# A fused encoder layer: softmax division on rows by VectorE and GpSimd, residual stores from ScalarE, embedding loads from GpSimd, the embedding stage's sums spread otherwise

## The chip, the cores and the metric

The kernel runs on one core of a Trainium2 chip. The metric is device time in microseconds (us). Its engines work from queues of their own: TensorE (PE in the profile, its weight loads PEld), VectorE (DVE), ScalarE (ACT), GpSimd (POOL) and SyncE (SP, which here only issues transfers). An engine takes its instructions strictly in the order of its queue, and a wait on a semaphore holds up everything queued behind it.

## The reference, cut to what matters

One layer over x of 1024 tokens by 1024 features, all in float32:

```
u    = x @ W_in                                # projection
R    = bidirectional retention, 8 heads        # chunks of 128 tokens
A    = windowed attention, 8 query heads, 2 key/value heads, 128 tokens to each side
       e = exp(scores - m);  probs = e / (sum(e) + exp(sink - m));  out = probs @ v
h    = LN1(alpha * x + concat(R * silu(gate), A) @ W_out)
f    = (silu(h @ W_gate) * (h @ W_up)) @ W_down + sigmoid(h @ W_pg) * (p @ W_pe)
out  = LN2(alpha * h + f)
```

The division `e / (...)` and the gated embedding `sigmoid(h @ W_pg) * (p @ W_pe)` are the two places that most of the change is about.

## The kernel before, in words

Matrices are multiplied in tiles of 128 x 128 by 128 x 512. Each float32 operand is split into a high part and the remainder (`split`: ScalarE copies, L79, VectorE subtracts, L80), and three multiplications make one product (`mm3`, L83 to L85; `mm3c`, L288 to L290). Large products use a scheme with 7 products of sums of quarter matrices instead of 8 products of quarters. So there are always sums of operands to be made by VectorE and GpSimd ahead of a product, and sums of results behind it.

The stages, in time: the first projection (to about 49 us), the other projections (49 to 171), retention and attention together (171 to 420), the out projection with LN1 (420 to 515), the gated embedding (`ple`, 515 to 602), gate and up products of the feed-forward part (602 to about 1040) and the down product with LN2 (to the end).

**Order.** In the projections, in `ple` and in the feed-forward part all five queues follow the order of the program text (`manual_schedule`). In the attention stage only TensorE does so; the other four are ordered by a scheduler that estimates times. In the out projection a scheduler orders all five.

**Projections.** The 7 products of a pair of weight tiles run as 6, 5, 2, 7, 4, 3 (with 1 earlier). Products 4 to 7 use sums of x, kept split in the tiles `TX`: two of them in a pool of their own (`T`), two in slots that keys (`k`) and queries (`q`, `v`) need later. After products 5, 2, 7 and 4 of the last pair, `keys` (L330 to L341) and `queries` (L343) build the split keys and queries of the attention.

**Attention.** There are 4 pairs of heads, and for each pair 8 blocks of 128 queries. `scores(n)` multiplies queries and keys into a bank (L671, L672); VectorE adds the distance term and takes the maximum (L673); ScalarE takes exp with the row sum (L677); VectorE takes the reciprocal of the sum (L679); GpSimd multiplies the identity matrix by it, which gives two diagonal matrices `dg` (L681). `turn(n)` then multiplies each 128 x 128 block of e by its `dg` (L690): one matmul that transposes the block and divides it. ScalarE copies the result to `ptr` (L692), and `values(n)` multiplies it by v (L702). TensorE runs `scores` two blocks ahead of `turn`; between them stand the steps of retention (`keys` L550, `kv` L564, `scan` L576 and L579, `scores` L589, `out` L609 to L620) and a queue of products from the other stages, cut in equal shares. Besides, GpSimd makes sums of the weights W_pg (`weight_sums`, L444 to L447, loaded by L442).

**Embedding.** `ple` runs the 7 products in the order 1, 2, 6, 7, 5, 4, 3, for rows 128 tokens at a time (k = 0 to 3). `to_T(t)` (t = 4 to 7) transposes a tile of h on TensorE into two banks (tags `t` and `o`, two buffers each) and makes three differences from it, x1, x2, x3 (L993, L995, L998), the split of one quarter (`put_h`, L883 and L884) and the split of x2 for product 6 (`put`, L978 and L979). `keep_h` scales h by alpha on ScalarE (L887) and stores it to `zd` (L888). `t3`, `t1`, `t4s` and `t4` make the operands of products 7, 5 and 4. `pg_load` loads a product's weights into the two `raw` buffers (L904), `pg_split` splits them (L912, L913). `plus` (L1079) and `gate` (L1073) add the results. `embed_next` multiplies a gate by its embedding (L1055), adds the result to `zd` by a transfer of GpSimd's queue (L1056), and fetches the next embedding into one of two buffers `pe` (`fetch`, L1046). In `prod(p, ..., side)` the functions in `side[k]` are called after the k-th row block. Then `ahead(2, ...)` prepares the feed-forward products; `Pair.load` brings their weights (L1120) into `raw` and `ln`.

Of the kernel before, what the change touches and what calls it, by code (L numbers as in the profile page):

```python
# [40 lines left out]
def layer(tc, xT, xn, w_first, w_mt, w_out, w_pg, w_pe, pT, w_gu, w_dn,  # L41
# [138 lines left out]
    TX = {n: tt([P, 2, 4, HF], f"T{n}", dt=F32R) for n in (4, 2)}  # L180
    TX[1] = [kt_("k", 4, (P, 2, HF)) for _ in range(4)]
    TX[3] = [kt_(*t, (P, 2, HF)) for t in (("q", 3), ("q", 3), ("q", 3), ("v", 1))]

    def tx(n, e, c):
        return TX[n][c][:, e, :] if n in (1, 3) else TX[n][:, e, c, :]

# [162 lines left out]
    with tc.manual_schedule(engines={ET.PE, ET.DVE, ET.Activation, ET.Pool, ET.SP}):  # L349
# [86 lines left out]
    def weight_sums(kt):  # L436
# [212 lines left out]
    class Attention:  # L649


        def __init__(self, i, y):
            self.i, self.y = i, y
            self.st, self.sc, self.pt, self.o, self.dg = {}, {}, {}, {}, {}

        def scores(self, n):
# [19 lines left out]
            for g in range(2):  # L676
# [3 lines left out]
            dg = self.dg[n] = bt([P, 2, P], "dg", 2)  # L680
            pool.tensor_tensor(dg, ident.unsqueeze(1).to_broadcast([P, 2, P]),  # L681
                               st_[:, 3, j, :].unsqueeze(2).to_broadcast([P, 2, P]), ALU.mult)

        def turn(self, n):
            lo, hi = span(n)
            self.pt[n] = []
            for g in range(2):
                tb = bank("t", (P, 4, P))
                for kb in range(hi - lo):
                    pe.matmul(tb[:, kb, :], self.sc[n][g][:, kb * P:(kb + 1) * P], self.dg[n][:, g, :], start=True, stop=True)  # L690
# [89 lines left out]
    with tc.manual_schedule(engines={ET.PE}):  # L780
        enqueue([spill(AQI[2]), spill(RKI[3]), embedding(0), spill(RQI[3]), embedding(1), gate(0), gate(1), gate(3)])
        turn_rv = rv_load(0)
        for i in range(NPAIR):
# [12 lines left out]
            ws = [(weight_sums, 2 * i), (weight_store, 2 * i), (weight_sums, 2 * i + 1), (weight_store, 2 * i + 1)] if i < 2 else [none] * 4  # L796
# [3 lines left out]
            else:  # L800
                first_steps = [val_last, K(0), X0, Q(0), F, C(0), X1, gat, F, K(1), sco(0), F]
            run(first_steps + [
                C(1), K(2), sco(1), F, C(2), K(3), F, trn(0), sco(2), F, C(3), (r.scan,), ws[0], val(0), F, trn(1), sco(3), F,
                val(1), Y(0, 0), F, trn(2), sco(4), F, val(2), Y(0, 1), N(0), ws[1], F, trn(3), sco(5), ws[2], F,
                val(3), Q(1), more[0], F, trn(4), sco(6), F, val(4), Y(1, 0), F, trn(5), sco(7), more[1], ws[3], F,
                val(5), Y(1, 1), N(1), F, trn(6), F, nt[0], nt[1], val(6), F, trn(7), F], 28)
# [79 lines left out]
    def keep_h(t):  # L886
        act.activation(accs[t], accs[t], AF.Copy, scale=ALPHA)  # L887
        sp.dma_start(zd[t], accs[t])  # L888
# [92 lines left out]
    def to_T(t):  # L981
# [16 lines left out]
        dve.tensor_tensor(x3, b1, x3, ALU.subtract)  # L998
        keep_h(t)
# [42 lines left out]
    def fetch():  # L1042
        if len(es_) < len(embs):
            t, h, _ = embs[len(es_)]
            e = ct([P, HF], "pe", 2)
            sp.dma_start(e, ed[t][:, hs[h]])  # L1046
# [13 lines left out]
    def ple(ahead):  # L1060
# [580 lines left out]
```

## Time and profile before

| | |
|---|---|
| median of 3 runs | 1255.15 us (1251.72 to 1260.1) |
| the profiled execution | 1257.43 us, of it a span of 1255.5 us from the first to the last instruction |
| mean granted clock of TensorE | 0.988 of full speed |
| busy, of the span | PE 1217.1, PEld 1008.4, DVE 774.7, ACT 511.6, POOL 497.4 us |
| transfers | 177 MB, mean 141 GB/s |

"Busy" counts the time in which an instruction of the engine runs. Matmuls overlap, each starting before the one ahead of it has ended. So what counts is the distance from one start to the next, and the gaps.

### The profile page before, as it was taken

How to read it: one execution, taken by the hardware profiler on the slowest of the kernel's cores; microseconds unless marked ns; L12 is line 12 of the kernel's file. 1: busy time of each engine (PE TensorE's matmuls, PEld its weight loads, DVE VectorE, ACT ScalarE, POOL GpSimd, SP SyncE). 2: the span in 40 equal slices, each digit the busy share in tenths (PEclk: the TensorE clock that was granted, in tenths of full speed). 3: DMA queues.
4: the chain of work that ended last, by engine and by line, in shares of the span. 5: the costliest groups of instructions: out<-in, count | busy, mean ns of one | idle time of the engine just before them, and what ended most of it. 6: DMA issues, size and time to landing. Idle time of an engine off the chain costs nothing.

```text
span 1255.5 us, 17085 instructions
## 1 busy us (share of the span) xinstructions
PE 1217.1 (97%) x6075; PEld 1008.4 (80%) x6075; DVE 774.7 (62%) x1294; ACT 511.6 (41%) x958; POOL 497.4 (40%) x455
## 2 busy tenths in 40 slices
PE   9999989999999999989799999999999999999997
PEld 7778868878888888768678888888888888888885
DVE  7854485767574538786555445555545556875668
ACT  5432354555565511463422333333233324652442
POOL 2553142432222002141565654665655714033226
PEclk9999989999999999999899999999999999999999
DMA  6223361542220333436643333222332249999987
GB/s 221 87 100 117 117 215 39 177 166 80 92 77 18 114 109 114 133 113 173 178 122 112 126 126 120 75 74 109 126 126 95 81 146 254 379 280 207 263 190 201
DMA packets 72677, 177.44 MB, mean 141 GB/s; under 512 B 8592, under 2 KB 10768, under 8 KB 72592
## 3 DMA queue, kind: packets, MB, share of 16 engines
q1 hardware_dynamic: 61648, 155.37, 35.3%
q0 software_dynamic: 10944, 20.98, 9.8%
q8 instruction: 48, 0.79, 0.3%
q14 instruction: 37, 0.30, 0.1%
HBM read 123.10 MB, written 47.97 MB: 136 GB/s over the span
## 4 chain that ended last, share of the span: by engine, by line
PE 79%; DVE 8%; DMA 5%; ACT 3%; issue 3%; POOL 1%; SPq 0%; DVEq 0%; ACTq 0%; POOLq 0%
PE bo L288 5%; PE bo L290 5%; PE bo L289 5%; PE bt L288 4%; PE bt L289 4%; PE bt L290 4%; PE bmm L290 4%; PE bmm L288 4%; PE bmm L289 4%; PE bs L288 4%; PE bs L290 4%; PE bs L289 4%; PE bmm L83 3%; PE bt L690 3%; PE bmm L84 3%; PE bmm L85 3%
## 5 line engine op out<-in xcount | busy, mean ns | idle before, releaser
L1158 POOL TENSOR_TENSOR ev<-ev 128x512 f32<-128x512 f32 x33 | 54.9, 1663 | 89.3 <-DVE ev L1173 36.3
L80 DVE TENSOR_TENSOR w<-H,w 128x512 fp32r<-128x512 f32 x44 | 40.6, 923 | 61.7 <-ACT w L79 61.7
L80 DVE TENSOR_TENSOR w<-raw,w 128x512 fp32r<-128x512 f32 x51 | 43.3, 862 | 38.0 <-ACT w L79 37.8
L1128 POOL TENSOR_TENSOR H<-ln 128x512 f32<-128x512 f32 x22 | 29.5, 1341 | 89.3 <-DMA ln<-in_w_gu 89.3
L1162 POOL TENSOR_TENSOR ev<-ev,ev 128x512 f32<-128x512 f32 x44 | 62.7, 1436 | 2.6
L1156 ACT ACTIVATE ev<-ev 128x512 f32<-128x512 f32 x33 | 20.9, 633 | 101.7 <-DVE ev L1173 101.7
L80 DVE TENSOR_TENSOR u<-H,u 128x512 fp32r<-128x512 f32 x47 | 35.9, 763 | 37.9 <-ACT u L79 37.6
L681 POOL TENSOR_TENSOR dg<-cst,st 128x256 f32<-128x256 f32 x32 | 21.4, 668 | 92.4 <-DVE st L679 77.7
L677 ACT ACTIVATE sc<-sc,st 128x385 f32<-128x385 f32 (+1 forms) x64 | 37.2, 583 | 37.9 <-DVE st L675 37.6
L80 DVE TENSOR_TENSOR u<-raw,u 128x512 fp32r<-128x512 f32 x32 | 38.8, 1215 | 18.8 <-ACT u L79 18.7
L690 PEld LDWEIGHTS bt<-dg,sc 128*128 128x128 f32 x352 | 44.0, 191 | 5.8 <-POOL dg L681 2.6
L83 PE MATMUL bmm<-H,w 128*128 128x512 f32 x112 | 48.2, 431 | 0.2 <-ACT H L79 0.2
L858 POOL TENSOR_TENSOR stt<-stt,cst 128x1 f32<-128x1 f32 x8 | 12.1, 1524 | 90.9 <-DVE stt L857 90.9
L79 ACT ACTIVATE u<-H 128x512 fp32r<-128x512 f32 x47 | 29.6, 630 | 43.9 <-PE bs L290 17.2
L690 PE MATMUL bt<-dg,sc 128*128 128x128 f32 x352 | 45.0, 276 | 1.6 <-POOL dg L681 1.4
L673 DVE CUSTOM_DVE_ANT_0 sc<-cst,bs,skb 128x384 f32<-128x384 f32 (+1 forms) x64 | 35.2, 576 | 15.8 <-PE bs L672 15.7
L84 PE MATMUL bmm<-H,w 128*128 128x512 f32 x112 | 44.5, 397 | 0.2 <-DVE H L80 0.2
L85 PE MATMUL bmm<-H,w 128*128 128x512 f32 x112 | 44.4, 396 | 0.0
L692 ACT ACTIVATE ptr<-bt 128x384 f32<-128x384 f32 (+1 forms) x64 | 29.1, 461 | 29.7 <-PE bt L690 29.0
L79 ACT ACTIVATE w<-raw 128x512 fp32r<-128x512 f32 x51 | 31.0, 624 | 20.6 <-DMA raw<-in_w_out 5.4
L1132 POOL TENSOR_TENSOR H<-raw,H 128x512 f32<-128x512 f32 x22 | 36.9, 1676 | 0.0
L79 ACT ACTIVATE w<-H 128x512 fp32r<-128x512 f32 x44 | 27.4, 622 | 23.1 <-PE bs L290 6.3
(893 smaller groups left out, 4120.9 us busy)
## 6 DMA issues: line engine op xcount, KB each, us to landing
ad<-ev SPq DMA_DIRECT2D x33, 512.0 KB, 2.9
raw<-in_w_gu SPq DMA_DIRECT2D x22, 512.0 KB, 4.6
ln<-in_w_gu SPq DMA_DIRECT2D x22, 512.0 KB, 3.7
raw<-ad SPq DMA_DIRECT2D x40, 256.0 KB, 5.8
ln<-ad SPq DMA_DIRECT2D x37, 256.0 KB, 6.5
H<-in_w_dn SPq DMA_DIRECT2D x33, 256.0 KB, 7.7
raw<-in_w_mt SPq DMA_DIRECT2D x12, 512.0 KB, 3.5
h<-in_w_dn POOLq DMA_DIRECT2D x24, 256.0 KB, 7.3
```

Source lines behind the costliest of these rows:

```text
L79: act.activation(hi, raw, AF.Copy)
L80: dve.tensor_tensor(lo, raw, hi.bitcast(F32), ALU.subtract)
L83: pe.matmul(o, lh, rh, start=start, stop=False)
L84: pe.matmul(o, lh, rl, start=False, stop=False)
L85: pe.matmul(o, ll, rh, start=False, stop=stop)
L288: pe.matmul(o, lh, rh, start=start, stop=False, skip_group_check=True)
L289: pe.matmul(o, lh, rl, start=False, stop=False, skip_group_check=True)
L290: pe.matmul(o, ll, rh, start=False, stop=stop, skip_group_check=True)
L677: act.activation(sc[g][:, :nk + 1], sc[g][:, :nk + 1], AF.Exp, bias=st_[:, 1, j, g:g + 1], accum_out=st_[:, 2, j, g:g + 1])
L690: pe.matmul(tb[:, kb, :], self.sc[n][g][:, kb * P:(kb + 1) * P], self.dg[n][:, g, :], start=True, stop=True)
L1158: pool.tensor_tensor(c[:, 1, :], c[:, 0, :], c[:, 1, :], ALU.mult)
L1162: pool.tensor_tensor(self.ev[dst][:, 0, :], left, right, op)
```

## The change

Four parts, in the order of the program:

1. Projections: the sums of x change places (product 6 reads from the key slots, product 5 from the query slots, product 7 from the pool `T`), and `keys` and `queries` are called one product earlier each.
2. Attention: `dg` is gone. The rows of e are divided in place, those of the second head (g = 1) by GpSimd and of the first by VectorE, and `turn` is a plain transposition. GpSimd's queue follows the program's order in this stage. `weight_sums` is cut into `weight_load` and `weight_sums`, which stand two or three steps apart, and the stores one or two steps behind.
3. Embedding: `to_T(4)` stands ahead of product 1; within `to_T` the copies by ScalarE come first and the split of x2 last; `keep_h` in `to_T` has its store issued by ScalarE. `t3`, `t1` and `t4` stand one product later, beside the product ahead of the one that needs them. Embeddings are fetched by GpSimd, and `embed_next` is called twice in each of products 7, 5 and 4, three times in product 3 and seven times in the feed-forward part (before: four times in each of products 5, 4 and 3, then after each feed-forward product). The first pair's weights are loaded in product 4.
4. Feed-forward: `embed_next` after the products k = 0, 1, 2, 4, 5, 7 and 9.

```diff
-    TX = {n: tt([P, 2, 4, HF], f"T{n}", dt=F32R) for n in (4, 2)}
-    TX[1] = [kt_("k", 4, (P, 2, HF)) for _ in range(4)]
-    TX[3] = [kt_(*t, (P, 2, HF)) for t in (("q", 3), ("q", 3), ("q", 3), ("v", 1))]
+    TX = {n: tt([P, 2, 4, HF], f"T{n}", dt=F32R) for n in (4, 3)}
+    TX[2] = [kt_("k", 4, (P, 2, HF)) for _ in range(4)]
+    TX[1] = [kt_(*t, (P, 2, HF)) for t in (("q", 3), ("q", 3), ("q", 3), ("v", 1))]
...
-                {5: lambda: keys(hs[0]), 2: lambda: keys(hs[1]), 7: lambda: queries(hs[0]),
-                 4: lambda: queries(hs[1])}.get(p, lambda: None)()
+                {6: lambda: keys(hs[0]), 5: lambda: keys(hs[1]), 2: lambda: queries(hs[0]),
+                 7: lambda: queries(hs[1])}.get(p, lambda: None)()
...
-            dg = self.dg[n] = bt([P, 2, P], "dg", 2)
-            pool.tensor_tensor(dg, ident.unsqueeze(1).to_broadcast([P, 2, P]),
-                               st_[:, 3, j, :].unsqueeze(2).to_broadcast([P, 2, P]), ALU.mult)
+            for g, e in ((1, pool), (0, dve)):
+                e.tensor_scalar(sc[g][:, :nk], sc[g][:, :nk], st_[:, 3, j, g:g + 1], None, ALU.mult)
...
-                    pe.matmul(tb[:, kb, :], self.sc[n][g][:, kb * P:(kb + 1) * P], self.dg[n][:, g, :], start=True, stop=True)
+                    pe.transpose(tb[:, kb, :], self.sc[n][g][:, kb * P:(kb + 1) * P], ident)
...
-    with tc.manual_schedule(engines={ET.PE}):
+    with tc.manual_schedule(engines={ET.PE, ET.Pool}):
...
-    def keep_h(t):
+    def keep_h(t, e=sp):
         act.activation(accs[t], accs[t], AF.Copy, scale=ALPHA)
-        sp.dma_start(zd[t], accs[t])
+        e.dma_start(zd[t], accs[t])
...
         act.activation(x3, b0, AF.Copy)
+        h = HB[1, 1][:, 0, :, cols(t)]
+        act.activation(h, b1, AF.Copy)
         dve.tensor_tensor(x1, b0, hi(0, 0, t), ALU.subtract)
         dve.tensor_tensor(x1, x1, lo(0, 0, t), ALU.subtract)
         dve.tensor_tensor(x2, b1, x1, ALU.subtract)
-        put_h(1, 1, t, b1)
+        dve.tensor_tensor(HB[1, 1][:, 1, :, cols(t)], b1, h.bitcast(F32), ALU.subtract)
+        dve.tensor_tensor(x3, b1, x3, ALU.subtract)
         put(2, x2, t)
-        dve.tensor_tensor(x3, b1, x3, ALU.subtract)
-        keep_h(t)
+        keep_h(t, act)
...
-            sp.dma_start(e, ed[t][:, hs[h]])
+            pool.dma_start(e, ed[t][:, hs[h]])
...
-        prod(1, b1, True, False, lambda k: act.activation(s1[k], b1[k], AF.Copy), [L(to_T, 4), L(to_T, 5), L(to_T, 6)])
+        to_T(4)
+        prod(1, b1, True, False, lambda k: act.activation(s1[k], b1[k], AF.Copy), [L(to_T, 5), [], L(to_T, 6)])
...
-        prod(2, b1, False, True, c00, [L(to_T, 7), L(t3, 4), L(t3, 5, 6), L(t3, 7)])
+        prod(2, b1, False, True, c00, [L(to_T, 7)])
...
-        prod(4, by, False, True, gate(s1, s1, by, 0, 1), [E, E, E, E])
+        prod(4, by, False, True, gate(s1, s1, by, 0, 1), [L(t4, 7), E + [lambda: pairs2[0].load(0)], [lambda: pairs2[0].load(1)], E])
...
-            embed_next()
+            if k in (0, 1, 2, 4, 5, 7, 9):
+                embed_next()
```

**TensorE in the attention.** The rows are the `turn` of the first pair's second block and the `scores` two blocks on, before and then after. `bt` and `bs` are banks, `sc` the rows of e, `cst` holds the identity matrix; x3 stands for three instructions.

```order
L690 MATMUL bt_1565<-dg_1470,sc_1454 128x128 x3
L690 MATMUL bt_1571<-dg_1470,sc_1455 128x128 x3
L671 MATMUL bs_1581<-k_1220,q_1266 128x384
L672 MATMUL bs_1581<-k_1222,q_1266 128x384
L671 MATMUL bs_1585<-k_1221,q_1267 128x384
L672 MATMUL bs_1585<-k_1223,q_1267 128x384
```

```order
L692 MATMUL bt_1561<-cst,sc_1454 128x128 x3
L692 MATMUL bt_1567<-cst,sc_1455 128x128 x3
L674 MATMUL bs_1577<-k_1203,q_1252 128x384
L675 MATMUL bs_1577<-k_1205,q_1252 128x384
L674 MATMUL bs_1581<-k_1204,q_1253 128x384
L675 MATMUL bs_1581<-k_1206,q_1253 128x384
```

The order stays the same; the operand `dg` has given way to the constant identity matrix.

**SyncE's queue in the embedding stage**, before and then after. `zd` is the stored residual, `raw` the weight buffers, `pe` the embeddings, `in_w_gu` the feed-forward weights; ws_74, ws_75, ws_73 are the weights of products 6, 7 and 5.

```order
L888 DMA zd<-acc_4310 128x1024
L904 DMA raw_4748<-ws_74 128x1024
L904 DMA raw_4749<-ws_74 128x1024
L888 DMA zd<-acc_4391 128x1024
L888 DMA zd<-acc_4477 128x1024
L888 DMA zd<-acc_4563 128x1024
L904 DMA raw_4883<-ws_75 128x1024
L904 DMA raw_4884<-ws_75 128x1024
L904 DMA raw_4969<-ws_73 128x1024
```

```order
L906 DMA raw_4770<-ws_74 128x1024
L906 DMA raw_4771<-ws_74 128x1024
L906 DMA raw_4883<-ws_75 128x1024
L906 DMA raw_4884<-ws_75 128x1024
L906 DMA raw_4959<-ws_73 128x1024
L906 DMA raw_4960<-ws_73 128x1024
```

The four stores have left SyncE's queue; further down, twelve `pe` loads that stood ahead of the first `in_w_gu` load have left it too.

**VectorE between the end of `to_T(7)` and product 7**, before and then after. L998 (L1001 after) is x3 of `to_T(7)`, L979 (L981) to `H_4679` is the split of x3 for product 7 and to `H_4677` that of x2 for product 6, L913 (L915) the weights of product 7, L1079 (L1083) the sum that frees a bank.

```order
L998 TENSOR_TENSOR H_4680<-bo_4850,H_4680 128x512
L979 TENSOR_TENSOR H_4679<-H_4680,H_4679 128x4x128 x4
L913 TENSOR_TENSOR u_4927<-raw_4883,u_4927 128x512
L913 TENSOR_TENSOR u_4928<-raw_4883,u_4928 128x512
L913 TENSOR_TENSOR u_4929<-raw_4884,u_4929 128x512
L913 TENSOR_TENSOR u_4930<-raw_4884,u_4930 128x512
L1079 TENSOR_TENSOR A_4925<-A_4686,bt_4921 128x512
```

```order
L1001 TENSOR_TENSOR H_4680<-bo_4850,H_4680 128x512
L981 TENSOR_TENSOR H_4677<-ln_4797,H_4677 128x4x128
L915 TENSOR_TENSOR u_4919<-raw_4883,u_4919 128x512
L915 TENSOR_TENSOR u_4920<-raw_4883,u_4920 128x512
L915 TENSOR_TENSOR u_4921<-raw_4884,u_4921 128x512
L915 TENSOR_TENSOR u_4922<-raw_4884,u_4922 128x512
L1083 TENSOR_TENSOR A_4917<-A_4686,bt_4913 128x512
L981 TENSOR_TENSOR H_4679<-H_4680,H_4679 128x4x128
```

The four splits of x3 no longer stand ahead of the first bank-freeing sum; one stands behind each of the four sums.

More of the change, by code (lines that the diff above doesn't have):

```diff
@@ L434, in layer, with weight_load @@
     wsums = {}
-    def weight_sums(kt):
+    def weight_load(kt):
         a, b = wsums[kt] = atile((P, 2, HF)), atile((P, 2, HF))
@@ L442, in weight_sums @@
                 sp.dma_start(t[:, h, :], w_pg[h, 2 * i + q][:, c])
+    def weight_sums(kt):
+        a, b = wsums[kt]
         a00, a10, a01, a11 = a[:, 0, :], a[:, 1, :], b[:, 0, :], b[:, 1, :]
@@ L653, in __init__ @@
             self.i, self.y = i, y
-            self.st, self.sc, self.pt, self.o, self.dg = {}, {}, {}, {}, {}
+            self.st, self.sc, self.pt, self.o = {}, {}, {}, {}
         def scores(self, n):
@@ L795, in layer @@
             none = (lambda: None,)
-            ws = [(weight_sums, 2 * i), (weight_store, 2 * i), (weight_sums, 2 * i + 1), (weight_store, 2 * i + 1)] if i < 2 else [none] * 4
+            ws = [(f, 2 * i + j) for j in range(2) for f in (weight_load, weight_sums, weight_store)] if i < 2 else [none] * 6
             nt = [(lambda h=h: hold["t"](h),) if i < 3 else none for h in range(2)]
@@ L802, in layer @@
             run(first_steps + [
[L803 to L806, printed above, removed]
+                C(1), K(2), sco(1), F, C(2), K(3), ws[0], F, trn(0), sco(2), F, C(3), (r.scan,), val(0), F, trn(1), sco(3), ws[1], F,
+                val(1), Y(0, 0), F, trn(2), sco(4), F, val(2), Y(0, 1), N(0), ws[2], F, trn(3), sco(5), ws[3], F,
+                val(3), Q(1), more[0], F, trn(4), sco(6), F, val(4), Y(1, 0), ws[4], F, trn(5), sco(7), more[1], F,
+                val(5), Y(1, 1), N(1), ws[5], F, trn(6), F, nt[0], nt[1], val(6), F, trn(7), F], 28)
             val_last = val(7)
@@ L1088, in ple @@
         s1 = quad()
-        prod(1, b1, True, False, lambda k: act.activation(s1[k], b1[k], AF.Copy), [L(to_T, 4), L(to_T, 5), L(to_T, 6)])
+        to_T(4)
+        prod(1, b1, True, False, lambda k: act.activation(s1[k], b1[k], AF.Copy), [L(to_T, 5), [], L(to_T, 6)])
         g = quad()
-        prod(2, b1, False, True, c00, [L(to_T, 7), L(t3, 4), L(t3, 5, 6), L(t3, 7)])
+        prod(2, b1, False, True, c00, [L(to_T, 7)])
         by = banks(TO)
         u2 = quad()
-        prod(6, by, True, False, plus(u2, s1, by), [L(t1, 4) + L(t4s, 4), L(t1, 5), L(t1, 6) + L(t4s, 5), L(t1, 7)])
+        prod(6, by, True, False, plus(u2, s1, by), [L(t3, 4), L(t3, 5) + L(t4s, 4), L(t3, 6), L(t3, 7) + [fetch, fetch]])
         u3 = quad()
-        prod(7, by, False, False, plus(u3, s1, by), [L(t4s, 6), L(t4, 4), L(t4s, 7) + L(t4, 5), [fetch, fetch]])
+        prod(7, by, False, False, plus(u3, s1, by), [L(t1, 4) + L(t4s, 5), L(t1, 5) + E, L(t1, 6) + L(t4s, 6), L(t1, 7) + E])
         b5 = banks(MS)
-        prod(5, b5, True, False, gate(u3, u3, b5, 4, 1), [L(t4, 6) + E, E, L(t4, 7) + E, E])
-        prod(4, by, False, True, gate(s1, s1, by, 0, 1), [E, E, E, E])
-        prod(3, b5, False, True, gate(u2, u2, b5, 4, 0), [E, E + [lambda: ahead(2, 2)], E, E + [lambda: ahead(2, 4)]])
+        prod(5, b5, True, False, gate(u3, u3, b5, 4, 1), [L(t4s, 7) + L(t4, 4), E, L(t4, 5), L(t4, 6) + E])
+        prod(4, by, False, True, gate(s1, s1, by, 0, 1), [L(t4, 7), E + [lambda: pairs2[0].load(0)], [lambda: pairs2[0].load(1)], E])
+        prod(3, b5, False, True, gate(u2, u2, b5, 4, 0), [E, E + [lambda: ahead(2, 2)], [], E + [lambda: ahead(2, 4)]])
     sarena = []
@@ L1216, in prep @@
         def prep():
-            if p == 1:
+            if p == 1 and n:
                 pr.load(m)
```

2 lines of the change are left out of this document (1 added, 1 removed).

## The prediction

> **What bounds the kernel now.** First the page's busy times by engine (share of the span, instructions).
>
> ```profile
> PE 1217.1 (97%) x6075; PEld 1008.4 (80%) x6075; DVE 774.7 (62%) x1294; ACT 511.6 (41%) x958; POOL 497.4 (40%) x455
> ```
>
> TensorE is busy 97% of the span and idle 3%, some 38 us. So a change can gain in two ways only: TensorE gets less to do, or one of its few waits goes. Hence the second view, TensorE's waits (line waited at, releaser; us in total, times, longest).
>
> ```profile
> PE bmm L288 <- ACT u L79: 7.0, 1, 7.0
> PE bt L288 <- DVE A L1079: 4.7, 1, 4.7
> PE bs L288 <- DVE ev L1173: 2.9, 1, 2.9
> PE bt L499 <- DVE A L275: 2.5, 1, 2.5
> PE bs L288 <- DVE A L269: 2.0, 1, 2.0
> PE bo L620 <- DVE kv L579: 1.9, 1, 1.9
> ...
> PE bt L690 <- POOL dg L681: 1.4, 2, 1.1
> PE bo L877 <- DVE H L998: 1.4, 1, 1.4
> ```
>
> Seven of these eight stand in the stages that the change touches; the third stands in the feed-forward part, 40 us behind the embedding. The third view gives the stages' busy times (PE, PEld, DVE, ACT, POOL, each with its instructions; granted clock, DMA share, GB/s), for the attention and the embedding with its edges:
>
> ```profile
> 171.00:420.00 249.00, 243.97 (x1797) 208.53 (x1798) 157.86 (x427) 135.82 (x322) 74.91 (x126) 0.99 0.32 110
> 510.00:650.00 140.00, 123.97 (x533) 100.58 (x532) 93.77 (x129) 57.46 (x97) 56.64 (x45) 0.94 0.54 151
> ```
>
> In the attention TensorE waits 5 us of 249: what is taken from its queue there is time gained, as long as the engines that feed it keep up, and VectorE has 91 us free, GpSimd 174. In the embedding TensorE is idle 16 us of 140, so there the waits count.
>
> **Attention: the transpositions.** Start-to-start distances on TensorE (start, duration, work):
>
> ```profile
> 267.50 1.50 PE L690 MATMUL bt<-dg,sc 128*128 128x128 f32 x12
> 268.76 0.42 PE L671 MATMUL bs<-k,q 128*128 128x384 f32 x1
> 290.08 1.03 PE L499 MATMUL bt<-cst,raw 128*128 128x128 f32 x8
> 291.04 0.88 PE L702 MATMUL bo<-ptr,v 128*64 128x128 f32 x12
> L690 PE MATMUL bt<-dg,sc x352: 270/275/377, 187.7 to 409.0; 128*128 128x128 f32 x176
> ```
>
> A turn of two heads and three blocks is six products and takes 12 records: 268.76 − 267.50 = 1.26 us, 0.21 a product. Eight transpositions of the same shape (by `cst`, the identity) take 8 records and 291.04 − 290.08 = 0.96 us, 0.12 each. The 352 records are 176 products, so the change removes 176 × 0.09 = **15.8 us**. The 0.96 contains the step to the next kind of product; were a transposition exactly half (0.105), it would be 18.5. I take 18.
>
> "TensorE: Matmul & The Clock Gate" of the Trainium skill, Part 4: PE-mode transpose, speaks against this: a transposition does not count as work for the gate that grants the clock, so a stretch of them should fall to a lower clock. The trace doesn't agree so far: the stretch that begins with the eight transpositions of 290.08 shows a clock of 1.00 (its row stands under the rivals, where the time is worked out).
>
> What is added: per block one scaling of 128 x 384 in place by VectorE and one by GpSimd, 32 each; GpSimd's `dg` goes.
>
> ```profile
> L675 DVE TENSOR_SCALAR st<-st x32: 155/169/1254, 183.0 to 400.6; 128x2 f32<-128x2 f32 x32
> L372 DVE CAST w<-raw x2: 421/424/427, 3.2 to 7.1; 128x512 fp32r<-128x512 f32 x2
> L164 POOL CAST masks<-mraw x1: 393/393/393, 71.0 to 71.0; 128x256 bf16<-128x256 f32 x1
> 240.51 1.28 POOL L444 TENSOR_TENSOR A<-A,A 128x512 f32<-128x512 f32 x1 [5.50 <-DMA A<-in_w_pg]
> ```
>
> The trace has neither scaling. On VectorE it lies between 0.17 (two columns) and 0.42 (512 columns): I take 0.35, 11 us in all beside 91 free. On GpSimd it lies between 0.39 (256 columns, one operand) and 1.28 (512, two): I take 0.8, near the middle, since 384 is; `dg` took 0.61. The chain from exp to `turn` thus grows by 0.8 − 0.6 = 0.2 us (−0.2 to +0.7). Does that reach TensorE?
>
> ```profile
> 185.16 0.61 POOL L681 TENSOR_TENSOR dg<-cst,st 128x256 f32<-128x256 f32 x1 [1.44 <-DVE st L679]
> 187.68 1.34 PE L690 MATMUL bt<-dg,sc 128*128 128x128 f32 x8
> 205.12 0.61 POOL L681 TENSOR_TENSOR dg<-cst,st 128x256 f32<-128x256 f32 x1 [3.28 <-DVE st L679]
> 212.61 1.50 PE L690 MATMUL bt<-dg,sc 128*128 128x128 f32 x12
> ```
>
> In the steady part `dg` is ready at 205.73 and used at 212.61: 6.9 us of slack, 176/32 × 0.1 = 0.6 less per block behind it. At a pair's first block it is 187.68 − 185.77 = 1.9 us. Both hold 0.7. The waits of this stage, 1.4 for `dg` (GpSimd sat 5.50 us ahead of a sum whose weights were not loaded, and `dg` queued behind it) and 1.9 at the scan (L579), should go when the loads stand two or three steps ahead of their sums and GpSimd no longer blocks: −3. Against it, GpSimd now runs in program order, so a late transfer holds up every scaling behind it; and 11 us more on VectorE can delay the scan at each of 4 pair starts. I set +3 for these, **net 0**, with ends −3 and +10 (4 pair starts at 2.5 us, the longest wait in this stage now).
>
> **End of the projections.** `queries` and `keys` start one product earlier, so VectorE's sums at L269 and L275 are due earlier against TensorE. Rows: window, its length, PE busy, clock, DMA share, GB/s.
>
> ```profile
> 168.00:174.00 6.00, 3.47 (x15) 0.80 0.73 250
> 174.00:180.00 6.00, 6.00 (x36) 0.64 0.96 359
> ```
>
> Two waits, 2.0 + 2.5 = 4.5 us, and behind them a low clock: 3.47 × 0.20 + 6.00 × 0.36 = 2.9 us. One product's work of VectorE is moved away from the end, but the weights and the next stage's loads still come at this point (DMA share 0.96). I take the waits down to 2 and half of the clock loss away: −2.5 − 1.5 = **−4** (ends −1, if only some clock comes back, and −6, with one wait of 1.4 left of the whole 7.4).
>
> **Embedding.** Four waits with the lowered clock behind three of them.
>
> ```profile
> 556.00:560.00 4.00, 2.84 (x7) 0.66 0.83 250
> 610.00:614.00 4.00, 4.00 (x11) 0.50 0.33 136
> 614.00:618.00 4.00, 3.93 (x15) 0.84 0.23 72
> 644.00:648.00 4.00, 4.00 (x14) 0.75 0.00 0
> ```
>
> Lost to the clock: 4 × 0.34 = 1.4; 4 × 0.50 + 4 × 0.16 = 2.6; 4 × 0.25 = 1.0. With the waits 1.4, 4.7, 7.0 and 2.9 the whole is 16.0 + 5.0 = **21 us**. Each has a cause in a queue:
>
> ```profile
> 531.16 15.29 SPq L888 DMA_DIRECT2D zd<-acc  x3
> 546.55 1.20 SPq L904 DMA_DIRECT2D raw<-ws  x2
> 538.05 2.99 POOL L913 TENSOR_TENSOR w<-raw,w 128x512 fp32r<-128x512 f32 x2 [17.77 <-ACT w L912]
> 551.24 2.43 ACT L912 ACTIVATE u<-raw 128x512 fp32r<-128x512 f32 x4 [1.60 <-DMA raw<-ws]
> 586.56 15.04 SPq L1046 DMA_DIRECT2D pe<-ed  x7
> 601.65 0.42 SPq L1120 DMA_DIRECT2D raw<-in_w_gu  x1
> 608.85 0.63 ACT L79 ACTIVATE u<-raw 128x512 fp32r<-128x512 f32 x1 [7.54 <-DMA raw<-in_w_gu]
> ```
>
> The wait at 557: SyncE stood 15.29 us with stores whose `acc` ScalarE had not yet scaled. Behind them stood product 7's weights, issued at 546.55 and usable at 551.24, and behind their splits on VectorE stood the sum (L1079) that frees the bank TensorE waited for. The buffers `raw` were free at 538.05 + 2.99 = 541.0. Without the stores the weights land at 541.0 + 4.7 = 545.7, 5.5 us earlier; and with the four splits of x3 no longer ahead of the sum, it comes before TensorE wants the bank. The wait at 609 is alike: seven fetches held SyncE until 601.65, the load took 608.85 − 601.65 = 7.2 us. After the change the load is issued when `raw` is free, some 12 us earlier, and lands about 597, ahead of TensorE's arrival at 608.85 + 0.63 − 7.0 = 602.5. The 1.4 for x3 of `to_T` goes because x3 is now wanted a product later; the 2.9 hangs on VectorE's embedding steps, now thinned out.
>
> What is late next: ScalarE issues four stores, and each waits for nothing but ScalarE's own scaling. GpSimd issues the fetches and the adds in one queue with the splits, so a fetch waiting for a buffer holds a split. And `to_T(4)` ahead of product 1 puts product 2's weights behind one more block of VectorE's work. I keep 3 of the 21 us: **−18** (ends −8, when the 557 and the 644 waits come back in another form, and −21).
>
> Here the Trainium skill has a rule that speaks against a gain ("Trainium Kernel Development and Optimization", Quick Reference, Key Constraints): transfers issued by several engines run on the same 16 DMA engines, and another issuer saves only issue time. By it moving stores and fetches is worth next to nothing; the row at 531.16 differs only in that this queue waits, which is not issue time.
>
> **The sum.** −18 + 0 − 4 − 18 = −40. The profiled execution took 1257.43 us, so 1217.4; the median of the runs lies 2.3 lower (1255.15), so **1215 us**.
>
> **The rivals.**
>
> 1. *Half of the attention's gain is lost* (20%). With 18 us less on TensorE the feeding engines have less time at each pair's start, and the scan or a scaling ends last. For it: VectorE goes from 157.86 to 169 of 231 us, and 1.9 us of slack there is thin. Against: 6.9 us in the steady part. Price +10: 1225.
> 2. *The change doesn't do what it says in the embedding* (17%): fetches and adds in GpSimd's queue hold up its splits as they held SyncE's loads, and the wait only changes its engine. For it: POOL's 17.77 us of waiting ahead of 538.05 shows that its queue is held by others already. Against: it is busy only 56.64 of 140 us. −8 in place of −18: 1225; none at all, 1233.
> 3. *Slower: transpositions do not hold TensorE's clock* (4%). Place: the `turn`s, 32 of them over the whole attention.
>
> ```profile
> 290.00:300.00 10.00, 9.73 (x82) 1.00 0.35 134
> ```
>
> For it: the row 174 to 180, at 0.64 while TensorE was busy all the time, in a stretch that opens with transpositions of L499 (though behind two waits). Against: this row, clock 1.00 with the eight of 290.08 among its 82 records. The attention's TensorE work would be 244 − 18 = 226 us; at a mean clock of 0.80 it takes 282 with 5 of waits 287, +38 against 249, and with −4 and −18 the whole is +16: 1271. The point from which it decides: 226 / c + 5 = 249 + 22, c = 0.85. This is the case in which the skill's page on the clock gate, cited above, would hold fully.
> 4. *A transposition costs as much as the product did* (4%), since the data are still float32. For it nothing but the type; against it the 8 records of 290.08. The 18 go: 1233.
>
> **How the numbers follow.** The forecast has 55%, its own range 1205 to 1223 by the ends of the terms. Rivals 1, 2 and 4 have 41% and reach 1225 to 1233, rival 3 has 4%. Low end: the projections' −6, the embedding's −21 and −3 in the attention and 18.5 for the transpositions together give 1207; the clock still missing in the attention (0.01 × 249 = 2.5 us) would make it 1204. High end 1237: both rivals 1 and 2 at once give 1235. About 1% is what a measurement of this kernel tells from no change. Faster than 1242.6: all but rival 3 and a mishap, 93%; within 1%: 4%; slower than 1267.7: 3%.
>
> **What the profile after would show.** If right: TensorE's `turn` has 176 records at a distance near 0.11 us, its busy time in the attention falls by about 18, clock still 0.99; the list of waits has no 7.0 and no 4.7; SyncE shows no block of 15 us between 520 and 610; the clock is near 1.00 through the embedding. VectorE's scaling shows a mean near 0.35 and GpSimd's near 0.8. Wrong, if `turn` has waits on either scaling at each block (the chain, not TensorE, bounds), if the clock falls in the attention, if waits on `pe` or on GpSimd's splits stand where those on `u` and A stood, or if the end of the projections is as late as before.

## The result and the profile after

The changed kernel takes **1246.9 us** (median of 20 runs) where the kernel before takes 1255.9 (20 runs): a ratio of 0.9926, 95% interval 0.9910 to 0.9943. That is 9 us less, not 40. The forecast of 1215 us and its range of 1204 to 1237 both missed.

The profiled execution took 1254.62 us (span 1252.8), the longest of the 20. A second profile of the same kernel (label d_all below) took 1247.82. The rows in this section are of the first, and the second agrees with them but for what is said.

Busy times of the changed kernel, to be held against the same row of before:

```profile
PE 1207.1 (96%) x5899; PEld 990.6 (79%) x5899; DVE 781.0 (62%) x1326; ACT 508.9 (41%) x958; POOL 524.9 (42%) x471
```

TensorE has 176 records less, and its busy time fell by 10 us only; GpSimd has 27 us more. TensorE's waits (line waited at, releaser; us, times, longest):

```profile
PE bs L592 <- DVE st L676: 6.8, 6, 1.7
PE bs L290 <- DVE u L80: 4.5, 1, 4.5
PE bs L288 <- DVE ev L1178: 2.8, 1, 2.8
PE bo L623 <- DVE kv L582: 2.6, 3, 1.3
...
PE bo L288 <- ACT h0b L980: 2.4, 2, 2.0
PE bmm L83 <- ACT w L79: 2.2, 1, 2.2
```

The waits of 7.0 and 4.7 us and the one for `dg` are gone, as forecast. In their place stand some twenty of 0.3 to 1.7 us in the attention, most of them on VectorE, and one of 4.5 us that was not there. New, too, are 2.4 us at operands of product 4 (L980): `t4` of the last tile is called in product 4 itself, not ahead of it, and TensorE waits 2.0 us for it.

**Attention.** The stretch from its first scores to its last values, before and then after (window, its length, then PE, PEld, DVE, ACT, POOL busy with their instructions, granted clock, DMA share, GB/s):

```profile
181.50:411.30 229.80, 225.78 (x1707) 193.37 (x1705) 147.69 (x409) 128.49 (x309) 69.49 (x122) 1.00 0.28 96
```

```profile
180.30:411.60 231.30, 212.85 (x1531) 174.42 (x1529) 159.39 (x442) 125.97 (x309) 98.89 (x130) 0.98 0.28 97
```

TensorE has 13 us less to do, and the stretch has the same length (230.1 in the second profile). The waiting has grown from 4 us to 18, and the clock is lower, 0.98. The `turn` itself does what it should:

```profile
192.13 0.82 PE L692 MATMUL bt<-cst,sc 128*128 128x128 f32 x6
192.70 0.42 PE L674 MATMUL bs<-k,q 128*128 128x384 f32 x1
```

Six transpositions take 0.57 us from start to start, where six products took 1.26: 0.115 us each, 176 × 0.115 = 20 us. The scalings cost more than I took:

```profile
L684 POOL TENSOR_SCALAR sc<-sc,st x32: 931/1463/1515, 184.4 to 406.3; 128x384 f32<-128x384 f32 x24, 128x256 f32<-128x256 f32 x8
L684 DVE TENSOR_SCALAR sc<-sc,st x32: 353/420/744, 184.5 to 406.2; 128x384 f32<-128x384 f32 x24, 128x256 f32<-128x256 f32 x8
```

In the median VectorE needs 0.42 us where I took 0.35, GpSimd 1.46 where I took 0.8, which is above my upper end of 1.28.

**Where a wait arises.** The first normalization of the retention is the clearest place. VectorE, and TensorE's step that needs the score banks (L589), before:

```profile
208.23 0.62 DVE L673 CUSTOM_DVE_ANT_0 sc<-cst,bs,skb 128x384 f32<-128x384 f32 x1
...
208.77 0.68 DVE L633 TENSOR_REDUCE sm<-sq 128x8 f32<-128x512 f32 x1
209.36 0.61 DVE L673 CUSTOM_DVE_ANT_0 sc<-cst,bs,skb 128x384 f32<-128x384 f32 x1
...
209.87 1.32 PE L589 MATMUL bs<-A,A 64*128 64x128 f32 x16
```

TensorE came to L589 at 209.87, when VectorE had just read the second bank (209.36 + 0.61). It did not wait, but it had no slack either, and no list of waits shows that. The same place after:

```profile
207.72 0.61 DVE L676 CUSTOM_DVE_ANT_0 sc<-cst,bs,skb 128x384 f32<-128x384 f32 x1
...
208.25 0.69 DVE L598 TENSOR_TENSOR qq<-A,qd 128x512 f32<-128x512 f32 x1
208.85 0.68 DVE L636 TENSOR_REDUCE sm<-sq 128x8 f32<-128x512 f32 x1
209.57 0.17 DVE L637 TENSOR_SCALAR sm<-sm 128x8 f32<-128x8 f32 x1
209.69 0.61 DVE L676 CUSTOM_DVE_ANT_0 sc<-cst,bs,skb 128x384 f32<-128x384 f32 x1
...
208.39 0.49 PE L592 MATMUL bs<-A,A 64*128 64x128 f32 x2 [0.80 <-DVE st L676]
210.36 1.81 PE L592 MATMUL bs<-A,A 64*128 64x128 f32 x14 [1.49 <-DVE st L676]
```

TensorE arrives earlier and waits twice, 0.80 and 1.49 us. VectorE's order has changed as well: between its two reads of the banks stand now three steps (L598, L636, L637), before one.

VectorE came to this place late, too. GpSimd's queue ahead of it, then ScalarE and VectorE, after:

```profile
197.10 1.47 POOL L684 TENSOR_SCALAR sc<-sc,st 128x384 f32<-128x384 f32 x1 [3.15 <-DVE st L682]
198.54 1.28 POOL L447 TENSOR_TENSOR A<-A,A 128x512 f32<-128x512 f32 x1
...
203.82 0.30 POOL L671 COPY sc<-skb 128x1 f32<-128x1 f32 x2
...
204.04 0.62 ACT L680 ACTIVATE sc<-sc,st 128x385 f32<-128x385 f32 x1 [3.56 <-POOL sc L671]
...
205.38 0.17 DVE L682 RECIPROCAL st<-st 128x2 f32<-128x2 f32 x1 [2.82 <-ACT sc L680]
```

L671 is a short copy by GpSimd that puts the sink's score into one more column of the row, and exp (L680) needs it. In program order it stands behind a scaling and four sums of W_pg, so ScalarE waits 3.56 us for it and VectorE 2.82 us at the reciprocal, ahead of the reads of the banks. ScalarE's waits for this copy in the attention, in the changed kernel and in k_prog (below), which is the longest of all:

```profile
ACT sc L680 <- POOL sc L671: 16.4, 5, 4.3
```

```profile
ACT sc L680 <- POOL sc L671: 26.8, 9, 4.4
```

Before the change there is no such wait. Four of the five in the changed kernel (3.5 to 4.3 us) stand behind the four groups of sums, in the first two pairs. There the waits of TensorE at L592 come in twos, 2.3 and 2.9 us together; in the other two pairs, which make no sums, they are 0.9 and 0.7.

Behind the second such place the granted clock falls:

```profile
268.00:272.00 4.00, 2.32 (x19) 1.00 0.29 103
272.00:276.00 4.00, 2.76 (x16) 0.52 0.31 102
276.00:280.00 4.00, 4.00 (x17) 0.63 0.82 291
```

That is 4.00 x 0.48 + 4.00 x 0.37 = 3.4 us of full clock lost; behind the first (208 to 216, at 0.84 and 0.74) it is 1.7 more. In d_all only the second place shows it.

**Behind the embedding.** GpSimd's queue, then VectorE and TensorE, after:

```profile
599.12 0.86 POOL L1050 DMA_DIRECT2D pe<-ed  x1
599.69 1.60 POOL L1133 TENSOR_TENSOR H<-ln 128x512 f32<-128x512 f32 x1
...
611.02 1.30 POOL L1137 TENSOR_TENSOR H<-raw,H 128x512 f32<-128x512 f32 x1
612.26 0.88 POOL L1060 DMA_DIRECT2D zd<-A  x1
612.85 0.86 POOL L1050 DMA_DIRECT2D pe<-ed  x1
...
617.61 0.69 DVE L1059 TENSOR_TENSOR A<-A,pe 128x512 f32<-128x512 f32 x1 [8.95 <-DMA pe<-ed]
...
618.96 0.80 PE L290 MATMUL bs<-H,u 128*128 128x512 f32 x1 [4.45 <-DVE u L80]
```

Eight sums of weights stand between two fetches, so the second fetch leaves at 612.85; VectorE waits 8.95 us for it, the split of `u` stands behind that, and TensorE waits 4.45 us for the split. From 590 to 600 the clock was 1.00; after this wait it is 0.54 for 4 us:

```profile
620.00:624.00 4.00, 4.00 (x12) 0.54 0.97 160
```

### The profile page after: what moved, and what is told of

Same layout as the page of the kernel before. It is cut to its first block, busy times and chain, and to the rows that moved or that the text cites. A ratio compares the mean times of both kernels' runs of the same rounds, so it can differ in the third digit from the quotient of the medians.

```text
span 1252.8 us, 16749 instructions
## 1 busy us (share of the span) xinstructions
PE 1207.1 (96%) x5899; PEld 990.6 (79%) x5899; DVE 781.0 (62%) x1326; ACT 508.9 (41%) x958; POOL 524.9 (42%) x471
## 4 chain that ended last, share of the span: by engine, by line
PE 77%; DVE 7%; issue 5%; DMA 4%; POOL 4%; ACT 3%; DVEq 0%; SPq 0%; ACTq 0%; POOLq 0%
PE bo L290 5%; PE bo L288 5%; PE bo L289 5%; PE bs L288 5%; PE bs L290 5%; PE bmm L288 5%; PE bmm L289 5%; PE bs L289 5%; PE bmm L290 5%; PE bt L290 4%; PE bt L288 4%; PE bt L289 4%; PE bmm L83 3%; PE bmm L84 3%; PE bmm L85 3%
## 5 line engine op out<-in xcount | busy, mean ns | idle before, releaser
L684 POOL TENSOR_SCALAR sc<-sc,st 128x384 f32<-128x384 f32 (+1 forms) x32 | 42.7, 1333 | 105.2 <-DVE st L682 96.1
L680 ACT ACTIVATE sc<-sc,st 128x385 f32<-128x385 f32 (+1 forms) x64 | 37.2, 584 | 47.2 <-DVE st L678 30.6
L83 PE MATMUL bmm<-H,w 128*128 128x512 f32 x112 | 48.5, 433 | 2.7 <-ACT w L79 2.2
L80 DVE TENSOR_TENSOR u<-raw,u 128x512 fp32r<-128x512 f32 x32 | 35.7, 1120 | 4.5 <-ACT u L79 4.5
L1134 POOL TENSOR_TENSOR H<-H,raw 128x512 f32<-128x512 f32 x22 | 35.1, 1595 | 1.7
L1283 POOL DMA_DIRECT2D H<-in_w_dn x11 | 9.6, 869 | 59.4 <-DMA H<-in_w_dn 53.1
L1283 POOL DMA_DIRECT2D h<-in_w_dn x24 | 21.3, 900 | 30.8 <-issue 18.6
```

The source lines that it names most:

```text
L80: dve.tensor_tensor(lo, raw, hi.bitcast(F32), ALU.subtract)
L83: pe.matmul(o, lh, rh, start=start, stop=False)
L680: act.activation(sc[g][:, :nk + 1], sc[g][:, :nk + 1], AF.Exp, bias=st_[:, 1, j, g:g + 1], accum_out=st_[:, 2, j, g:g + 1])
L684: e.tensor_scalar(sc[g][:, :nk], sc[g][:, :nk], st_[:, 3, j, g:g + 1], None, ALU.mult)
```

## The experiments

Each was timed against the kernel before in the same series of runs; "stretch" is the time from the attention's first scores to its last values in the profile.

**The three parts alone.** d_att has the change's part 2 alone, d_emb parts 3 and 4, d_proj part 1; d_all is the changed kernel.

```diff
 # d_att: L436 to L447, L681, L690 and the lists of steps as changed
 # d_emb: keep_h, to_T, fetch, the side lists of prod and the FF positions of embed_next as changed
 # d_proj:
-    TX = {n: ... for n in (4, 2)}
+    TX = {n: ... for n in (4, 3)}
-                {5: lambda: keys(hs[0]), 2: lambda: keys(hs[1]), ...
+                {6: lambda: keys(hs[0]), 5: lambda: keys(hs[1]), ...
```

> The kernel before with the change's attention part alone (scaling of the rows, plain transpositions, GpSimd in program order, the loads of W_pg ahead of their sums); projections and embedding as before. Theory A (TensorE's gain is given back inside this stage, because the chain of VectorE, GpSimd and ScalarE sets its length): 1252 to 1258 us, TensorE's work in the stage some 15 us less and its waits some 12 us more. Theory B (this part gains by itself and loses it only beside the other parts): 1240 us or less.

> The kernel before with the embedding and feed-forward parts alone (parts 3 and 4). If the fetches of embeddings behind GpSimd's sums give back what the freed SyncE queue brings: 1248 to 1251 us, with a wait of 4 to 5 us some 18 us behind the first feed-forward product, on a VectorE that waits for pe. If this part brings what was forecast: 1238 us.

> The kernel before with the projections' part alone (part 1). As forecast: 4 us less, 1252 us, with the stretch from the last projection to the attention's first scores some 5 us shorter; if the weights' wait that the changed kernel shows at this place takes the gain, 1255 us.

> The changed kernel itself, once more, as the mark for the parts: 1245 to 1250 us. If the parts add up, its gain is the sum of the three others; the profile shows which of the changed kernel's stretches were those of a slow single execution (the start of the program at a clock of 0.6 to 0.8 above all).

Measured: d_att 1252.1 us (ratio 0.9969, 0.9951 to 0.9988), d_emb 1249.0 (0.9955, 0.9935 to 0.9974), d_proj 1254.3 (0.9994, 0.9978 to 1.0010), d_all 1247.8 (0.9951, 0.9931 to 0.9972). Between series the ratio is the safer measure, since the kernel before took 1253.7 to 1256.0 us in them. The parts add up within their intervals (3 + 6 + 1 us against 7 to 9), so theory B falls: the attention loses its gain inside its own stretch (232.2 us in d_att, TensorE idle 17 of them). d_proj starts its first scores at 179.0 in place of 181.5, and the waits at L269 and L275 give way to one of 2.2 us at the splits of the last weights (L83); in the time this can't be told from nothing.

**What in the attention takes the gain.** All start from the changed kernel. g_noscale leaves out the scaling, g_act gives VectorE's half to ScalarE, g_psched lets the scheduler order GpSimd's queue again, h_ps_noscale and h_ps_act join these.

```diff
 # g_noscale, h_ps_noscale
-            for g, e in ((1, pool), (0, dve)):
-                e.tensor_scalar(sc[g][:, :nk], sc[g][:, :nk], st_[:, 3, j, g:g + 1], None, ALU.mult)
 # g_act, h_ps_act, in place of VectorE's half
+            act.activation(sc[0][:, :nk], sc[0][:, :nk], AF.Copy, scale=st_[:, 3, j, 0:1])
 # g_psched and all h_ps kernels
-    with tc.manual_schedule(engines={ET.PE, ET.Pool}):
+    with tc.manual_schedule(engines={ET.PE}):
```

> The changed kernel without the scaling of the rows on either engine (the division is left out; the rest as changed). Theory A1 (the added work, 14 us on VectorE and 43 us on GpSimd, takes TensorE's gain): 1234 to 1238 us, the attention's stretch from its first scores to its last values near 217 us, in place of 230. Theory A2 (VectorE's older steps, the score rows and the normalization of the retention, were just in time before and set the pace of these stretches, whatever is added): 1242 to 1246 us, the stretch 225 us or more, with waits of TensorE at L592 and L623 of the same size.

> The changed kernel with the first head's rows scaled by ScalarE in place of VectorE (ScalarE is busy 136 of 249 us in this stage). A1 with VectorE as the engine that counts: 1240 us or less. A2: within 3 us of the changed kernel, 1244 to 1250 us.

> The changed kernel with GpSimd's queue of the attention ordered by the scheduler again, as before the change. If GpSimd's program order costs TensorE its gain (theory A3): 1240 us or less. If that order is without effect or helps: 1246 to 1253 us, with a wait at GpSimd's sums of W_pg back.

> GpSimd's queue of the attention ordered by the scheduler, and no scaling of the rows at all (the division is left out). With the scheduler's order the stretch was 224.0 us with the scaling. Theory A1 (what is left of the loss is the added work): about 216 us, 1235 us in all. Theory A2 (what is left is VectorE's older steps, above all the scan and the normalization): 220 to 223 us, 1239 to 1243 us, and the longest waits of TensorE stand at the scan's readers (L623) again.

> GpSimd's queue of the attention ordered by the scheduler, the first head's rows scaled by ScalarE. A1: VectorE has 14 us less, 1238 to 1240 us. A2: 1242 to 1246 us, as with VectorE's scaling in this order.

Measured: g_noscale 1239.9 us (0.9871, 0.9848 to 0.9894), g_act 1247.3 (0.9934, 0.9912 to 0.9955), g_psched 1243.3 (0.9905, 0.9883 to 0.9926), h_ps_noscale 1238.5 (0.9849, 0.9815 to 0.9882), h_ps_act 1243.2 (0.9890, 0.9861 to 0.9919). The stretches of d_all, g_noscale, g_psched and h_ps_noscale, in this order:

```profile
178.50:408.60 230.10, 211.41 (x1531) 173.00 (x1529) 159.12 (x442) 125.69 (x309) 98.89 (x130) 0.99 0.28 98
```

```profile
177.00:401.60 224.60, 211.60 (x1531) 175.82 (x1529) 147.41 (x410) 126.59 (x310) 55.98 (x96) 0.98 0.30 101
```

```profile
180.30:404.40 224.10, 209.50 (x1531) 172.12 (x1530) 155.32 (x443) 126.58 (x310) 90.45 (x122) 0.99 0.30 102
```

```profile
179.90:397.90 218.00, 207.74 (x1531) 172.01 (x1529) 141.91 (x411) 126.38 (x309) 47.32 (x88) 0.99 0.30 102
```

Read as a table of two by two, the stretch is 5.5 and 6.1 us shorter without the scaling, 6.0 and 6.6 without GpSimd's program order. The times give 8 and 5 us for the scaling, 4 and 1 for the order (the 1 is not clear of nothing, as the intervals of g_noscale and h_ps_noscale overlap); one profile's stretch is good to some 3 us, since the same attention took 224.1 in g_psched and 227.6 in h_ps_late (below). So A1 and A3 are both true in part and neither alone: the scaling costs 5 to 8 us, the order 1 to 6. With both taken away the stretch is 218, against 229.8 − 20 = 210 that the transpositions alone would give. A1 in the form that VectorE's time counts is not borne out: ScalarE in its place changes nothing (229.9 and 223.3 us), though ScalarE stands in the same chain and could lose what VectorE wins. The program order works through VectorE: in g_psched its two reads of the banks stand together again,

```profile
206.68 0.61 DVE L676 CUSTOM_DVE_ANT_0 sc<-cst,bs,skb 128x384 f32<-128x384 f32 x1
...
207.22 0.61 DVE L676 CUSTOM_DVE_ANT_0 sc<-cst,bs,skb 128x384 f32<-128x384 f32 x1
```

and of the waits at L592 0.2 us are left. That the scheduler orders VectorE otherwise because it reckons with GpSimd's fixed order is the likely reason, but only argued. The other path is in the traces: ScalarE's waits for the copy L671, 16.3 us in d_all, are 1.8 in g_psched. In g_noscale, which keeps the program order and the sums but not the scalings, there are none. So that wait takes both, the order and the scaling in it, and the two costs overlap. What the scaling costs in the scheduler's order (5 us) has another reason.

**The older steps.** h_ps_dve2 has both scalings on VectorE, h_ps_ym the normalization's last multiplication on GpSimd, both with the scheduler's order.

```diff
 # h_ps_dve2
-            for g, e in ((1, pool), (0, dve)):
-                e.tensor_scalar(sc[g][:, :nk], ...
+            for g in (0, 1):
+                dve.tensor_scalar(sc[g][:, :nk], ...
 # h_ps_ym
-            dve.tensor_tensor(ym, ym, sm[:, 2, :]...
+            pool.tensor_tensor(ym, ym, sm[:, 2, :]...
```

> GpSimd's queue of the attention ordered by the scheduler, both heads' rows scaled by VectorE (0.42 us each in place of 1.4 on GpSimd). If GpSimd's slow scaling costs: stretch 220 us or less, 1238 to 1240 us. If VectorE's time costs: 228 us or more, 1246 us. If neither: 1243 us.

> GpSimd's queue of the attention ordered by the scheduler, and the last multiplication of the retention's normalization on GpSimd behind its power, where VectorE waited for that power (11.7 us in 8 waits). Theory A2 (VectorE's in-order waits in older steps set the pace): the stretch 3 to 6 us shorter, 1238 to 1241 us. A1: no change, 1243 us.

Measured: h_ps_dve2 1245.7 us (0.9913, 0.9880 to 0.9947), stretch 226.6; h_ps_ym 1238.2 (0.9861, 0.9820 to 0.9902), stretch 218.8. So GpSimd's slow scaling isn't the cost by itself: on VectorE the same work costs no less (g_psched has 1243.3 and 224.1; neither difference is clear of noise). But A2 holds for a part: VectorE's wait for GpSimd's power in the normalization, in g_psched

```profile
DVE ym L639 <- POOL sm L638: 13.1, 8, 1.8
```

was as long before the change (12.9 us) and cost nothing then (k_dg below); without it and the multiplication the time is now some 5 us less and the stretch 5.3. The intervals of the two times still overlap, and the move takes off VectorE 7 us of work as well as the wait, so the two are not told apart.

**The embeddings.** f_sp has their loads on SyncE again; f_late and f_wide move the seven late ones.

```diff
 # f_sp
-            pool.dma_start(e, ed[t][:, hs[h]])
+            sp.dma_start(e, ed[t][:, hs[h]])
 # f_late, h_ps_late; then f_wide
-            if k in (0, 1, 2, 4, 5, 7, 9):
+            if k in (3, 4, 5, 6, 7, 8, 9):
+            if k in (3, 6, 9, 12, 15, 18, 21):
```

> The changed kernel with the embeddings' loads issued by SyncE again; their number per product and all else as changed. Theory E1 (the wait of 4.4 us behind the first feed-forward product comes from these loads standing behind GpSimd's sums of weights): that wait goes, 1241 to 1244 us. Rival E2 (SyncE stands at these loads again and holds the feed-forward weights): the wait at the first feed-forward product is back with 3 to 7 us, 1247 us or more.

> The changed kernel with the seven late embeddings after the feed-forward products 3 to 9 in place of 0, 1, 2, 4, 5, 7 and 9. E1' (VectorE's wait for an embedding that GpSimd fetches behind its sums of weights holds up the splits): the waits of TensorE of 4.4 and 2.8 us behind the first feed-forward product go, with the clock behind them, 1240 to 1242 us. If the wait moves along with the embeddings: 1245 to 1249 us and the same waits some 14 us later.

> Both at once: GpSimd's queue of the attention ordered by the scheduler and the late embeddings after products 3 to 9. If the two are independent and both theories hold, 1237 us; if only the first does, 1243 us.

> The changed kernel with the seven late embeddings after the feed-forward products 3, 6, 9, 12, 15, 18 and 21. Theory E3 (with two buffers a fetch leaves only when VectorE has freed one, and lands some 5 us later; embeddings closer than that make VectorE wait, and its splits with it): three products are 14 us, so the waits of 4.4, 2.8 or 8.4 us go but for what stands without embeddings: 1240 to 1243 us. If the waits have another cause (the feed-forward operands themselves): 1246 to 1249 us.

Measured: f_sp 1246.4 us (0.9935, 0.9907 to 0.9963), f_late 1247.6 (0.9931, 0.9910 to 0.9953), h_ps_late 1243.3 (0.9886, 0.9856 to 0.9916), f_wide 1237.5 (0.9855, 0.9806 to 0.9904). TensorE's longest wait in f_sp (it has one of 3.4 us at a split beside it), and SyncE's queue ahead of it; then the longest in f_late:

```profile
PE bs L288 <- DVE ev L1178: 7.5, 1, 7.5
...
601.08 19.45 SPq L1050 DMA_DIRECT2D pe<-ed  x6
```

```profile
PE bs L288 <- DVE ev L1178: 9.3, 2, 8.4
```

Another issuer, or later places, only move the wait, and each time it has another cause. In the changed kernel the fetch stands behind eight sums, as E1 says. In f_sp SyncE stands 19.45 us at six fetches, and the feed-forward weights behind them are issued at 620.62 only: this is E2's mechanism, at 1246.4 us. In f_late the fetches leave in time but land 7.1 and 8.9 us later (610.89 to 617.98 and 614.86 to 623.80), where the median of all 16 is 4.6. In f_wide the longest wait behind the first feed-forward product is 1.2 us, near the program's end, and the time is 10 us below the changed kernel's, more than E3 asked for. VectorE's waits for an embedding are 18.3 us in the changed kernel, 12.5 in f_late and 4.4 in f_wide, and in f_wide none of them reaches TensorE. So the distance decides, as E3 says: with two buffers a late fetch stops VectorE with all its splits, unless the embeddings stand far enough apart. That more buffers would do the same was not tried.

**Both together.** h_ps_ym_wide is h_ps_ym with f_wide's places. k_dg has part 2 undone in it, k_prog GpSimd's program order.

```diff
 # k_dg: L681 and L690, GpSimd's queue and the sums of W_pg as before the change
 # k_prog
+    with tc.manual_schedule(engines={ET.PE, ET.Pool}):
```

> The same with the late embeddings three products apart, as the version that may be the best: 1235 us if A2 and E3 hold both, 1239 us if one of them does.

> The best version (1229 us) with the attention part undone: diagonal matrices, products, GpSimd's queue and the sums of W_pg as before; the normalization's last multiplication on GpSimd and the late embeddings three products apart are kept. If VectorE's wait was what took the transpositions' gain, the stretch of the attention is 227 to 230 us and the whole 1238 to 1241 us. If the moved multiplication alone brought it, 220 us and 1230 us.

> The best version (1229 us) with GpSimd's queue of the attention in program order, as in the changed kernel. If that order cost only through VectorE's wait for the power: 1228 to 1231 us, the stretch 219 to 221 us. If it costs by itself: 1233 us or more, 223 us or more.

Measured: h_ps_ym_wide **1228.9 us** (0.9782, 0.9746 to 0.9817), faster than both kernels, 6 us better than expected and 9 below h_ps_ym in the same series; k_dg 1238.1 (0.9860, 0.9811 to 0.9908); k_prog 1242.2 (0.9898, 0.9853 to 0.9942). Their stretches in this order:

```profile
179.20:398.20 219.00, 207.96 (x1530) 172.05 (x1528) 150.25 (x435) 126.61 (x310) 98.15 (x130) 0.99 0.30 102
```

```profile
178.80:409.40 230.60, 224.89 (x1707) 193.41 (x1705) 143.71 (x403) 129.02 (x310) 76.40 (x130) 1.00 0.29 98
```

```profile
178.20:412.50 234.30, 211.91 (x1531) 173.17 (x1529) 153.16 (x434) 125.82 (x309) 104.20 (x138) 0.99 0.28 96
```

The moved multiplication without the transpositions brings nothing (230.6), the transpositions without it and in program order nothing (230.1), both with the scheduler's order 11 us. k_prog takes the second of its two expectations and goes beyond it: it is the longest of all. In program order the multiplication joins the power in GpSimd's queue, and the stretch grows by 5 us over f_wide's 229.3. So the program order costs by itself, not only through VectorE's wait for the power; ScalarE's waits for the copy L671 are 26.8 us here and 3.5 in h_ps_ym_wide.

## Why the prediction was wrong, point by point

**What bounds the kernel.** "What is taken from its queue there is time gained, as long as the engines that feed it keep up" was right, and the condition after the comma decided. I tested it with sums over the stage (VectorE 91 us free), and that is the step that failed. The engines were free on average and just in time at some twenty places, each of them good for 0.3 to 1.7 us.

**Transpositions, −18.** Right, rather too small: 20 us by starts. TensorE's busy time in the stretch fell by 13 only, since the clock was lower behind the new waits, by 5 us in this profile and 3.4 in d_all; in h_ps_noscale and h_ps_ym_wide, with fewer waits, it fell by 18.

**Waits of the attention, net 0 (−3 to +10).** This is the first term that was mis-sized: waits rose from 4 to 18 us, **+14**, beyond its end, and the clock behind them took the 5 us just named. I read the slack at two chosen instructions of one chain (6.9 and 1.9 us, of `dg`) and not at the others TensorE waits for. GpSimd's program order, which I listed as a risk for the scalings behind a late transfer, takes 1 to 6 us; what it held up in the trace was the copy ahead of exp, behind sums and scalings (16.4 us of ScalarE's waits), a step that I had left out of the chain. The scaling takes 5 to 8 us, partly through this same wait; why it costs 5 in the scheduler's order too, wherever its halves were put, is open. Of what remains, the normalization's last multiplication on VectorE, with the wait for the power, takes some 5 (1243.3 to 1238.2).

**Projections, −4.** The two waits shrank and the clock from 174 to 180 came back (1.00 for 0.64), but the wait for the split of the last weights (2.2 us) took their place: 2.5 us in the profile of d_proj, 1 us and not clear of nothing in its time.

**Embedding, −18 (−8 to −21).** The second mis-sized term: the part alone brings 6 us. Both causes that I named in SyncE's queue were right, and the waits of 7.0 and 4.7 us are gone. But I kept 3 us for new waits, and rival 2 came: the new one behind GpSimd's sums, 4.5 us with its lowered clock, and the 2.8 at L1178 that I took for thinned out. The 2.4 us at product 4's operands came on top, a wait that I had not looked for. f_wide brings 10 us more, so about 16 of the 21 were there to be had.

**Rivals.** Two of the four came at once: 1 (half of the attention's gain lost; nearly all of it was) and 2. I let the range end where each takes about 10 us; with what each part brought alone (3 us of 18, 6 of 18, 1 of 4) the sum is 1215 + 15 + 12 + 3 = 1245, next to the measured 1247. The forecast's own range was worked out wrongly as well: the ends of the terms give 1207 to 1240, not 1205 to 1223. Rival 4 is refuted by the 0.095 us of a transposition (0.57 / 6). Rival 3 too, though its sign, a clock that falls in the attention, did show at 208 and 272. The granted clock in the later part of the attention, after, then in h_ps_ym_wide at the time of the second fall, with the same transpositions and no waits:

```profile
300.00:420.00 120.00, 113.54 (x807) 1.00 0.21 72
```

```profile
260.00:280.00 20.00, 20.00 (x163) 1.00 0.47 165
```

So the falls stand behind waits, though not behind every one, and not behind transpositions as such. The rule of "TensorE: Matmul & The Clock Gate" of the Trainium skill (Part 4: PE-mode transpose), by which transpositions don't count as work for the clock, does not show at this density: 1.00 in both rows. The other rule that I cited, of "Trainium Kernel Development and Optimization" (Quick Reference, Key Constraints), that the issuing engine of a transfer saves only issue time, fits better than I allowed: f_sp and d_all, which differ in the issuer of 16 loads, take 1246.4 and 1247.8 us. What counted in these runs was what the issuer has to get through first, six fetches in f_sp and eight sums in d_all.

## What to carry to other kernels

Before work is taken from the busiest engine, ask at each place where it meets another engine how late that other one may be: compare the end of what it needs with its own start, before the change, since slack of zero is in no list of waits. A shared buffer pair sets a distance between its uses (here a fetch landed 4.6 us after it left in the median and 8.9 at worst); moving its loads to another queue or later only moved the wait, and setting them further apart removed it. And an order that is fixed on one engine can put a short step that others wait for behind long work, and can go with another order on other engines, so look at both.

## What the runs showed of the hardware that was not expected

GpSimd needed 1.47 us to scale 128 x 384 in place (197.10 of the profile after), more than for each of the four sums of 128 x 512 behind it (1.26 to 1.30). And VectorE's split, a subtraction of two operands, is slowed beside GpSimd's sums. In f_late, a sum on GpSimd, a split on VectorE beside it, and another while GpSimd only issues transfers:

```profile
603.00 1.75 POOL L1137 TENSOR_TENSOR H<-raw,H 128x512 f32<-128x512 f32 x1
603.52 1.78 DVE L80 TENSOR_TENSOR w<-H,w 128x512 fp32r<-128x512 f32 x1
...
609.82 0.68 DVE L80 TENSOR_TENSOR u<-H,u 128x512 fp32r<-128x512 f32 x1
```

The same kind of split takes 0.68 us alone and 1.78 beside GpSimd's sums: it ends 0.55 us after GpSimd's instruction (605.30 against 604.75). GpSimd's sum is slower as well, 1.75 us against the 1.28 at 198.54 above, where VectorE was idle. "SBUF — State Buffer" of the Trainium skill (Terms) has a rule for this, that the two engines share a pair of ports and the loser is blocked for a full instruction; the trace agrees, as the split's end is about its own length behind GpSimd's. In the attention VectorE's time apart from its scalings did not grow (145 us against 148 before), so its busy time shows nothing of this kind there; whether GpSimd is held up was not tried.
